# A hybrid layer on one core: a gate tile, RWKV's clamp and masks, and the start of attention change their place

## The chip, the cores and the metric

The kernel runs on one core of a Trainium2 chip, as one launch. The metric is the device time of one execution in microseconds, the median of some runs. The engines meant below are TensorE (PE: matmuls and transposes), VectorE (DVE), ScalarE (ACT), GpSimd (POOL) and SyncE (SP), which only issues transfers. Each engine takes its instructions in the order in which they were built; they wait for each other through semaphores.

## The reference

One decoder layer over 1024 tokens of width 1024, all in float32. Two mixers work beside each other on the same normalized input, are weighed by sigmoid gates, and a SwiGLU feed-forward follows:

```python
p = rmsnorm(x, norm1_g) @ w_in           # RWKV columns | q, k, v | indexer columns | 2048 gate columns
ya = rwkv7_mix(token_shift(p_rwkv, mu))  # 8 heads of 64, state carried over all tokens
yb = dsa_attention(q, k, v, q_idx, k_idx, w_idx)   # 8 heads, 256 keys chosen for each query
m  = sigmoid(ga) * (ya @ w_o_rwkv) + sigmoid(gb) * (yb @ w_o_att)
h  = x + m @ w_out
z  = rmsnorm(h, norm2_g); u = z @ w_ffn_in
out = rmsnorm(h + (silu(u_gate) * u_up) @ w_ffn_out, normf_g)    # 2816 inner columns
```

The lines above are a digest with shortened names. In RWKV the key is divided by its norm, `kk / maximum(norm(kk), 1e-12)`, ahead of the scan over tokens.

## The kernel before, in words

Everything is held transposed, channels on the partitions and tokens along a row, in two halves of 512 tokens. A float32 product is made of three matmuls in a faster format: each operand is split into a high part (a copy by ScalarE, `split`, L114) and the rest (a subtraction by VectorE, L115), and `mm3` (L140, L141, L145) adds high x high, high x low and low x high. One output tile of a projection from 1024 channels is thus 24 matmuls of 128x512. `mm3_last` (L156) orders them so that the last k tile of the activations is read last.

The order of TensorE is written by hand; the order of the other engines comes from a scheduler that goes by dependencies and priorities. Dense work stands as generators in a queue, `fill`, and `pump(n)` draws about n matmuls of it wherever the code of RWKV would leave TensorE without work; `ticks` does so in small portions. RWKV's first quarters have attention and gate projections as their filling, the later ones the merge and the feed-forward of the first half.

RWKV goes in four quarters q of 256 tokens. In each the key's squares are summed by matmuls (`sums`, L587), VectorE clamps the sums into `nq` (L604), TensorE turns them (L608), VectorE takes two columns of eight into `nr` (L610), POOL raises them to the power -0.5 (L614), and after a split and another turn (L619) ScalarE copies `nrT` (L621), which L627 spreads over the channels. Then 64 products of 64x128 (L682) are masked by VectorE into eight tiles `MT`, two for each chunk c of four (L686), and TensorE turns B and K (L701), which ScalarE copies into `NAT` (L704). The first block of each mask is inverted on VectorE (`W`, L720 and L722), goes through memory (`d_w`, L724) and comes back as `TT` (L733) and, turned, `TZ` (L736), which L750 and L771 use ahead of the scan.

`att0` makes the gates of the second half: sixteen tiles of 24 matmuls, `proj_gates(1, ...)`, of which the first 64 matmuls are drawn before attention over the first half (`attend(0, ...)`), the rest in turn with it. Attention loads keys (L1036), values (L1040) and queries (L1048) through POOL's queue, multiplies them (L1062), takes the row maximum on VectorE (L1064), turns the weights (L1076) and applies them to the values (L1086).

At q=2, ahead of the L682 products, `ready()` runs what is left in `fill`, gives the buffers of `u1` (the normalized input of the second half) back, opens `zp0`, and draws the first step of `merge(0)`: eight tiles of ya and yb (256 KB each) are read back over SP and split into yhi and ylo. From then on `fill` holds the products of the merge with w_o, which begin behind the L701 of q=2, then those with w_out and the feed-forward.

At the end of the first half the last group of the feed-forward's way out (`ffn_out`, group 2, six k tiles) writes into h and adds up its squares (`Rms.add`, L234 and L235); `finish_out` does the same for the second half, in two parts of 256 tokens. `Rms.columns` (L241, L244) sums over the channels by matmuls with ones, and `spread` (L254) brings the result onto all partitions.

Of the kernel before, what the change touches and what calls it, by code (L numbers as in the profile page):

```python
# [11 lines left out]
F32 = mybir.dt.float32  # L12
# [37 lines left out]
def block_kernel(ctx: ExitStack, tc: tile.TileContext, ins: dict, outT: bass.AP, stop=None, dbg=None):  # L50
# [65 lines left out]

    wq = [SY]
# [102 lines left out]

    class Rms:


        def __init__(self, h, tok=slice(0, HT)):
            self.h, self.tok, self.n = h, tok, (tok.stop - tok.start) // 128
            self.acc = tp.tile([128, HT], F32, tag="sacc", name="sacc", bufs=2)

        def add(self, k):
            n = 128 * self.n
            if k == 0:  # L230
                A.activation(self.acc[:, :n], self.h[:, 0, self.tok], AF.Square)
            else:
                sq = tmp()
                A.activation(sq[:, :n], self.h[:, k, self.tok], AF.Square)  # L234
                V.tensor_tensor(self.acc[:, :n], self.acc[:, :n], sq[:, :n], op=ALU.add)  # L235

        def columns(self, rs2=None):

            ss, n = mix(), self.n
            for t in range(n):  # L240
                T.matmul(ss[:, 2 * t:2 * t + 2], self.acc[:, t * 128:(t + 1) * 128], ones[:, 0:2],  # L241
                         start=True, stop=True)
            rs = cp.tile([128, 4], F32, tag="rs", name="rs", bufs=1)
            V.tensor_scalar(rs[:, :n], ss[:, 0:2 * n:2], 1.0 / D, 1e-6, op0=ALU.mult, op1=ALU.add)  # L244
# [282 lines left out]
    def rwkv(half, p, consts, ready=None):  # L527
# [5 lines left out]
        for q in range(2 * half, 2 * half + 2):  # L533
# [14 lines left out]
            pump((64, 36, 24, 34)[q])  # L548
# [50 lines left out]
            V.tensor_tensor(km, km, k, op=ALU.mult)  # L599
# [4 lines left out]
            V.tensor_scalar(nq.rearrange("p a b -> p (a b)"), ps, 1e-24, None, op0=ALU.max)  # L604
            pump(14)
            ps = mix()
            for t in range(2):
                T.transpose(ps[:, t * 128:(t + 1) * 128], nq[:, t, :], ident)  # L608
            nr = p.tile([128, 16], F32, tag="nr", name="nr")
            V.tensor_copy(nr.rearrange("p (t c e) -> p t c e", t=2, c=4),  # L610
                          ps[:, 0:256].rearrange("p (t c k) -> p t c k", t=2, c=4)[:, :, :, 0:2])
# [4 lines left out]
            pump((24, 26, 22, 26)[q])  # L616
# [4 lines left out]
            A.activation(nrT, ps[0:16, 0:256], AF.Copy)  # L621
            pump(10)
# [51 lines left out]
            for c in range(4):  # L674
                pr, pa = divmod(c, 2)
                m = p.tile([128, 8, 128], F32, tag=f"x{c}", name="MT")
                pss = [mix(), mix()]
                for hh in range(4):
                    for g in range(2):
                        h = 2 * hh + g  # L680
                        ct, ro = h // 2, slice((h % 2) * 64, (h % 2) * 64 + 64)
                        T.matmul(pss[g][:, hh * 128:(hh + 1) * 128],  # L682
                                 BK[ct // 2][ro, ct % 2, pr, 2 * pa:2 * pa + 2, :].rearrange("p s t -> p (s t)"),
                                 AR[ro, ct, c, :, :].rearrange("p s t -> p (s t)"), start=True, stop=True)
                for g in range(2):
                    V.tensor_tensor(m[:, g::2, :], pss[g].rearrange("p (h t) -> p h t", h=4),  # L686
                                    cmask[:, 64 - 64 * pa:192 - 64 * pa].unsqueeze(1).to_broadcast([128, 4, 128]),
                                    op=ALU.mult)
                MT.append(m)
                ba = 64 - 64 * pa  # L690
                for b in range(2):
                    i0 = (c * 2 + b) * 8
                    SY.dma_start(d_n[q][i0:i0 + 8].rearrange("h s t -> s h t"),
                                 m[ba + 32 * b:ba + 32 * b + 32, :, ba + 32 * b:ba + 32 * b + 32])
            NAT = []
            for pr in range(2):
                n = p.tile([128, 2, 512], F32, tag=f"x{4 + pr}", name="NAT")
                for pa in range(2):
# [5 lines left out]
                    A.activation(n[:, pa, :], ps, AF.Copy)  # L704
                NAT.append(n)

# [37 lines left out]
            ticks((211, 236, 281, 241)[q], (13, 4, 10, 6)[q])  # L744
# [520 lines left out]
    def ffn_out(half, zp, f, gi, sqs=None):  # L1265
# [42 lines left out]
    def finish_out(half, zp, f):  # L1308
# [6 lines left out]
        with tc.tile_pool(name="wf", bufs=8, side="left", reuse_waits="tile") as wf:  # L1315
            ws, before = [], None
            for o in range(0, HT, 256):
# [6 lines left out]
                for d in range(8):  # L1324
# [8 lines left out]
                    sq.add(d)  # L1333
# [24 lines left out]
    for half in (1, 0):  # L1358
        st, up = opened("left", f"up{half}")
        su.append(st)  # L1360
        us.insert(0, act_tiles(up, f"u{half}"))
# [38 lines left out]
    def att0():  # L1400
# [3 lines left out]
        gates = proj_gates(1, us[1], range(16))  # L1404
        for _ in range(16):
# [37 lines left out]
    sz0.close()  # L1443
    finish_out(1, zp1, f1[0])
# [80 lines left out]
```

## Time and profile before

| what | before |
|---|---|
| median of 3 runs | 1742.55 us (1739.08 to 1746.03) |
| profiled execution | 1741.15 us |
| its span | 1739.4 us |
| mean granted clock of TensorE | 0.993 |
| TensorE busy | 1706.6 us, 98% |
| VectorE busy | 1123.0 us, 65% |
| ScalarE busy | 846.9 us, 49% |
| GpSimd busy | 98.5 us, 6% |

The span is the time from the first to the last instruction in the trace. A row of a timeline gives start, duration, engine, line, operation, operands and count, and in brackets the idle time of the engine before it with what ended it. A row of the waits gives total, number of times and longest. Matmuls overlap, so from row to row the difference of the starts counts, not the duration of one. A row of the windows gives the busy time of each engine, then TensorE's granted clock, the share of busy DMA engines and GB/s. Profiled lines are those of the kernel before.

### The profile page before, as it was taken

The numbers are of one execution on the slowest core, as the hardware profiler recorded it, in microseconds if no ns is written. First come the engines' busy times: TensorE is split into PE (matmuls) and PEld (weight loads), VectorE is DVE, ScalarE is ACT, GpSimd is POOL, SyncE is SP. The second block draws the span as 40 slices with busy tenths as digits, with TensorE's granted clock in tenths as the row PEclk, the third lists the DMA queues.
The fourth block names the chain that finished last, engine by engine and source line by source line (L and its number), as shares of the span: only waits on it lengthen the run. The fifth ranks groups of instructions, "written<-read, shape, count | busy, mean of one in ns | idle before, by whom it ended". The sixth has DMA issues, their size and how long they took to land.

```text
span 1739.4 us, 26865 instructions
## 1 busy us (share of the span) xinstructions
PE 1706.6 (98%) x10156; PEld 1407.9 (81%) x10156; DVE 1123.0 (65%) x2189; ACT 846.9 (49%) x1627; POOL 98.5 (6%) x123
## 2 busy tenths in 40 slices
PE   8999999999999998999999999999999999999997
PEld 6888888778778777878788888888788888888887
DVE  6789989957567457957877655445566564454464
ACT  6355898553544688755334455533234332232241
POOL 0000000000021111001000311000000000000000
PEclk9999999999999999999999999999999999999998
DMA  5452334435357535643343864263464344434442
GB/s 211 155 154 85 98 108 146 158 96 174 104 180 202 147 113 164 202 147 118 104 122 116 237 159 132 69 222 110 164 218 135 100 146 154 136 96 149 136 128 86
DMA packets 144001, 247.16 MB, mean 142 GB/s; under 512 B 49232, under 2 KB 72464, under 8 KB 143744
## 3 DMA queue, kind: packets, MB, share of 16 engines
q1 hardware_dynamic: 120512, 171.61, 31.5%
q10 hardware_dynamic: 15552, 47.75, 8.6%
q0 software_dynamic: 7808, 26.09, 5.6%
q8 instruction: 80, 1.31, 0.3%
q14 instruction: 49, 0.40, 0.1%
HBM read 192.40 MB, written 53.00 MB: 141 GB/s over the span
## 4 chain that ended last, share of the span: by engine, by line
PE 78%; DVE 9%; ACT 6%; issue 3%; DMA 3%; POOL 0%; SPq 0%; ACTq 0%; DVEq 0%; POOLq 0%
PE acc L140 20%; PE acc L145 19%; PE acc L141 19%; PE acc L156 3%; PE mix L1086 2%; PE mix L1062 2%; PE mix L1076 2%; ACT junk L977 2%; DVE wlo L115 1%; ACT junkl L977 1%; PE mix L927 1%; DVE junk L974 1%; DMA wst<-in_w_ffn_in 1%; ACT whi L114 1%; PE acc L1230 1%
## 5 line engine op out<-in xcount | busy, mean ns | idle before, releaser
L115 DVE TENSOR_TENSOR wlo<-wst,whi 128x1024 fp32r<-128x1024 f32 (+1 forms) x229 | 276.2, 1209 | 275.2 <-PE acc L145 124.2
L114 ACT ACTIVATE whi<-wst 128x1024 fp32r<-128x1024 f32 (+1 forms) x229 | 238.1, 1042 | 232.5 <-PE acc L141 175.5
L140 PE MATMUL acc<-zhi,whi 128*128 128x512 f32 x672 | 264.7, 394 | 0.0
L141 PE MATMUL acc<-zlo,whi 128*128 128x512 f32 x672 | 262.0, 390 | 0.0
L145 PE MATMUL acc<-zhi,wlo 128*128 128x512 f32 x672 | 170.2, 392 | 0.0
L140 PEld LDWEIGHTS acc<-zhi,whi 128*128 128x128 f32 x672 | 126.2, 188 | 26.9 <-issue 1.7
L141 PEld LDWEIGHTS acc<-zlo,whi 128*128 128x128 f32 x672 | 126.2, 188 | 24.8
L145 PEld LDWEIGHTS acc<-zhi,wlo 128*128 128x128 f32 x672 | 124.7, 188 | 25.5 <-issue 0.7
L140 PE MATMUL acc<-u1hi,whi 128*128 128x512 f32 x352 | 141.0, 401 | 0.1
L141 PE MATMUL acc<-u1lo,whi 128*128 128x512 f32 x352 | 138.0, 392 | 0.0
L140 PE MATMUL acc<-u0hi,whi 128*128 128x512 f32 (+1 forms) x352 | 135.3, 387 | 1.8 <-DVE tmp L333 1.8
L141 PE MATMUL acc<-u0lo,whi 128*128 128x512 f32 (+1 forms) x352 | 133.7, 382 | 0.0
L140 PE MATMUL acc<-fhi,whi 128*128 128x512 f32 (+1 forms) x318 | 114.0, 367 | 2.0 <-ACT whi L114 1.0
L141 PE MATMUL acc<-flo,whi 128*128 128x512 f32 (+1 forms) x318 | 112.9, 364 | 0.2 <-DVE flo L115 0.2
L145 PE MATMUL acc<-u1hi,wlo 128*128 128x512 f32 x352 | 90.5, 397 | 0.0
L145 PE MATMUL acc<-u0hi,wlo 128*128 128x512 f32 (+1 forms) x352 | 86.5, 385 | 0.0
L114 ACT ACTIVATE fhi<-tmp 128x512 fp32r<-128x512 f32 x44 | 27.8, 631 | 114.1 <-DVE tmp L1262 114.1
L140 PEld LDWEIGHTS acc<-u0hi,whi 128*128 128x128 f32 x352 | 66.2, 188 | 15.3 <-ACT stg L114 2.2
L140 PEld LDWEIGHTS acc<-u1hi,whi 128*128 128x128 f32 x352 | 66.4, 189 | 14.4 <-issue 0.9
L145 PEld LDWEIGHTS acc<-u1hi,wlo 128*128 128x128 f32 x352 | 65.5, 190 | 14.0 <-issue 0.9
L141 PEld LDWEIGHTS acc<-u1lo,whi 128*128 128x128 f32 x352 | 66.5, 189 | 12.6
L141 PEld LDWEIGHTS acc<-u0lo,whi 128*128 128x128 f32 x352 | 66.2, 188 | 12.2
(330 smaller groups left out, 3223.4 us busy)
## 6 DMA issues: line engine op xcount, KB each, us to landing
wst<-in_w_ffn_in SPq DMA_DIRECT2D x72, 512.0 KB, 3.6
wst<-in_w_in ACTq DMA_DIRECT2D x36, 512.0 KB, 4.3
wst<-in_w_in SPq DMA_DIRECT2D x27, 512.0 KB, 3.9
wst<-in_w_fo SPq DMA_DIRECT2D x25, 512.0 KB, 4.0
k<-d_k POOLq DMA_DIRECT2D x24, 512.0 KB, 8.2
h<-in_xT SPq DMA_DIRECT2D x32, 256.0 KB, 5.2
d_g<-tmp ACTq DMA_DIRECT2D x32, 256.0 KB, 3.4
tmp<-d_g SPq DMA_DIRECT2D x32, 256.0 KB, 3.4
```

What stands on the lines that cost most here:

```text
L114: A.activation(hi, x, AF.Copy)
L115: V.tensor_tensor(lo, x, hi.bitcast(F32), op=ALU.subtract)
L140: T.matmul(ps, whi[:, wk + k, :], ahi[:, ak + k, tok], start=k == 0, stop=False)
L141: T.matmul(ps, whi[:, wk + k, :], alo[:, ak + k, tok], start=False, stop=False)
L145: T.matmul(ps, wlo[:, wk + k, :], ahi[:, ak + k, tok], start=False, stop=k == nk - 1)
L156: T.matmul(ps, w[:, k, :], a[:, k, tok], start=k == 0 and w is whi and a is ahi, stop=k == nk - 1 and a is alo)
L927: T.matmul(ps[:, :w], iq[:, h, :], ik[:, i, c:c + w], start=i == 0, stop=i == 1)
L974: V.tensor_scalar(junk[:, :n], y, z[:, i:i + 1], None, op0=ALU.is_ge, op1=ALU.add, accum_out=cnt[:, i:i + 1])
L977: A.activation(junka[:, :n], y, AF.Sign, bias=z[:, i:i + 1], accum_out=cnt[:, i:i + 1])
L1062: T.matmul(ps[:, :w], q[bi // 2][:, e, bi % 2 * 128:bi % 2 * 128 + 128], k[:, i, e, c:c + w], start=i == 0, stop=i == 1)
L1076: T.transpose(ps[:, j * 128:(j + 1) * 128], L[:, (c + j) * 128:(c + j + 1) * 128], ident)
L1086: T.matmul(py[64 * e:64 * e + 64, bi * 128:(bi + 1) * 128], v[:, j, 64 * e:64 * e + 64], pts[e][j // 4][:, j % 4, :], start=j == b, stop=j ...
```

## The change

1. The clamp `nq`, the copies `nr`, `nrT` and `NAT`, and the masks `MT` get a high priority in the scheduler (`urgent`), and the key multiply is put behind the clamp.
2. The numbers of the pumps in RWKV shift a little; in the second half (q=2 and q=3) there is a pump of two matmuls behind the masks of every chunk (`pump(2 * half)`; a step of filling is four, so it draws one behind the first and the third chunk), and the one ahead of the products grows from 10 to 14.
3. `att0` draws ten steps of gates (40 matmuls), not sixteen (64), before attention begins, and has fifteen gate tiles. The ticks of q=1 fall by 24.
4. The sixteenth gate tile goes behind `ready()`, ahead of the merge in `fill`, so that it lies among the products and turns of q=2 and beside the load of y. `u1` stays for so long, and its buffers become those of m, later f and z.
5. The merge splits the first four tiles of y in its first step and the last four in a second one, which the code of RWKV draws behind the last mask and the last NAT copy (`ready_y`).
6. The last group of `ffn_out` orders the matmuls of its first tile by `mm3_last`.
7. At the very end the last square isn't added by VectorE, but goes into the sums by matmuls of its own.

```diff
+    def urgent():
+        return tc.high_priority()
...
+    class Slots:
+        def __init__(self, pools):
+            self.pools = pools
+        def tile(self, shape, dt, tag, name):
+            return self.pools[tag].tile(shape, dt, tag=tag, name=name)
...
-        def add(self, k):
+            self.parts = [self.acc]
+        def add(self, k, last=False):
...
+            elif last:
+                self.parts.append(tmp())
+                A.activation(self.parts[1][:, :n], self.h[:, k, self.tok], AF.Square)
...
-            ss, n = mix(), self.n
-            for t in range(n):
-                T.matmul(ss[:, 2 * t:2 * t + 2], self.acc[:, t * 128:(t + 1) * 128], ones[:, 0:2],
-                         start=True, stop=True)
+            n, ps = self.n, self.parts
+            sss = [mix() for _ in range(n if len(ps) > 1 else 1)]
+            for x in ps:
+                for t in range(n):
+                    T.matmul(sss[t % len(sss)][:, 2 * t:2 * t + 2], x[:, t * 128:(t + 1) * 128], ones[:, 0:2],
+                             start=x is ps[0], stop=x is ps[-1])
...
-            pump((64, 36, 24, 34)[q])
+            pump((60, 36, 24, 34)[q])
...
-            V.tensor_tensor(km, km, k, op=ALU.mult)
...
-            V.tensor_scalar(nq.rearrange("p a b -> p (a b)"), ps, 1e-24, None, op0=ALU.max)
+            with urgent():
+                clamp = V.tensor_scalar(nq.rearrange("p a b -> p (a b)"), ps, 1e-24, None, op0=ALU.max)
+            with tc.issue_after(clamp.ins):
+                V.tensor_tensor(km, km, k, op=ALU.mult)
...
-            pump((24, 26, 22, 26)[q])
+            pump((28, 26, 22, 38)[q])
...
-            pump(10)
+            pump(10 if half == 0 else 14)
...
-                    V.tensor_tensor(m[:, g::2, :], pss[g].rearrange("p (h t) -> p h t", h=4),
-                                    cmask[:, 64 - 64 * pa:192 - 64 * pa].unsqueeze(1).to_broadcast([128, 4, 128]),
-                                    op=ALU.mult)
+                    with urgent():
+                        masked = V.tensor_tensor(
+                            m[:, g::2, :], pss[g].rearrange("p (h t) -> p h t", h=4),
+                            cmask[:, 64 - 64 * pa:192 - 64 * pa].unsqueeze(1).to_broadcast([128, 4, 128]), op=ALU.mult)
                 MT.append(m)
+                pump(2 * half)
...
-                    A.activation(n[:, pa, :], ps, AF.Copy)
+                    with urgent():
+                        last = A.activation(n[:, pa, :], ps, AF.Copy)
                 NAT.append(n)
+            if q == 2:
+                with tc.issue_after(masked.ins), tc.issue_after(last.ins):
+                    ready_y()
...
-            ticks((211, 236, 281, 241)[q], (13, 4, 10, 6)[q])
+            ticks((211, 212, 281, 241)[q], (13, 4, 10, 6)[q])
...
-        mt = act_tiles(zp, "m", ("s2", "s3"))
         for j in range(8):
             t = ylo[:, j, :].bitcast(F32)
             SY.dma_start(t, (d_ya if j < 4 else d_yb)[half][j % 4])
-            split(yhi[:, j, :], ylo[:, j, :], t)
-        yield -30
+        for j in range(4):
+            split(yhi[:, j, :], ylo[:, j, :], ylo[:, j, :].bitcast(F32))
+        yield -20
+        for j in range(4, 8):
+            split(yhi[:, j, :], ylo[:, j, :], ylo[:, j, :].bitcast(F32))
+        yield -10
+        mt = act_tiles(zp, "m", ("s2", "s3"))
...
-        pss = []
-        if not final:
-            pss = [acc(), acc()]
-            yield from mm3_last(pss, [w(d) for d in range(2)], f, gn)
+        pss = [acc() for _ in range(1 if final else 2)]
+        yield from mm3_last(pss, [w(d) for d in range(len(pss))], f, gn)
...
-                    sq.add(d)
+                    sq.add(d, last=d == 7 and o > 0)
...
-        gates = proj_gates(1, us[1], range(16))
-        for _ in range(16):
+        gates = proj_gates(1, us[1], range(15))
+        for _ in range(10):
             yield next(gates)
...
-        su.pop().close()
-        zps.append(opened("left", "zp0"))
-        m = merge(0, zps[0][1], z0)
+        sz, zp = opened("left", "zp0")
+        zp = Slots({"s0": zp, "s1": zp, "s2": up1, "s3": up1})
+        zps.append((sz, zp))
+        m = merge(0, zp, z0)
         next(m)
-        fill.append(chain(m, ffn(0, zps[0][1], z0, f0)))
+        zps.append(m)
+        fill.append(chain(proj_gates(1, us[1], range(15, 16)), m, ffn(0, zp, z0, f0)))
...
-    rwkv(1, rp, consts, ready)
+    rwkv(1, rp, consts, ready, lambda: next(zps[1]))
```

More of the change, by code (lines that the diff above doesn't have):

```diff
@@ L237, in columns @@
         def columns(self, rs2=None):
-            ss, n = mix(), self.n
-            for t in range(n):
-                T.matmul(ss[:, 2 * t:2 * t + 2], self.acc[:, t * 128:(t + 1) * 128], ones[:, 0:2],
-                         start=True, stop=True)
+            n, ps = self.n, self.parts
[4 more added lines that the diff above has]
+                             start=x is ps[0], stop=x is ps[-1])
             rs = cp.tile([128, 4], F32, tag="rs", name="rs", bufs=1)
-            V.tensor_scalar(rs[:, :n], ss[:, 0:2 * n:2], 1.0 / D, 1e-6, op0=ALU.mult, op1=ALU.add)
+            m = len(sss)
+            for t, ss in enumerate(sss):
+                V.tensor_scalar(rs[:, t:n:m], ss[:, 2 * t:2 * n:2 * m], 1.0 / D, 1e-6, op0=ALU.mult, op1=ALU.add)
             if rs2 is None:
@@ L525, in rwkv_consts, with rwkv @@
         return cmask, wup, gup, rmask, ind, ind16
-    def rwkv(half, p, consts, ready=None):
+    def rwkv(half, p, consts, ready=None, ready_y=None):
         cmask, wup, gup, rmask, ind, ind16 = consts
@@ L685, in rwkv @@
                 for g in range(2):
[L686 to L688 removed]
+                    with urgent():
+                        masked = V.tensor_tensor(
+                            m[:, g::2, :], pss[g].rearrange("p (h t) -> p h t", h=4),
+                            cmask[:, 64 - 64 * pa:192 - 64 * pa].unsqueeze(1).to_broadcast([128, 4, 128]), op=ALU.mult)
                 MT.append(m)
+                pump(2 * half)
                 ba = 64 - 64 * pa
@@ L703, in rwkv @@
                                     ident)
-                    A.activation(n[:, pa, :], ps, AF.Copy)
+                    with urgent():
+                        last = A.activation(n[:, pa, :], ps, AF.Copy)
                 NAT.append(n)
+            if q == 2:
+                with tc.issue_after(masked.ins), tc.issue_after(last.ins):
+                    ready_y()
             N = p.tile([128, 32, 32], F32, tag="x6", name="N")
@@ L1360, in block_kernel @@
         su.append(st)
-        us.insert(0, act_tiles(up, f"u{half}"))
+        us.insert(0, act_tiles(up, f"u{half}", ("s2", "s3") if half else None))
+        if half:
+            up1 = up
     sb, bp = opened("right", "bp")
```

7 lines of the change are left out of this document (4 added, 3 removed).

## The prediction

> **What bounds the kernel now.** I read the page first, then the waits of TensorE, then the timeline of each place that the change touches.
>
> ```profile
> span 1739.4 us, 26865 instructions
> ...
> PE 1706.6 (98%) x10156; PEld 1407.9 (81%) x10156; DVE 1123.0 (65%) x2189; ACT 846.9 (49%) x1627; POOL 98.5 (6%) x123
> ```
> ```profile
> PE mix L701 <- DVE MT L686: 3.3, 1, 3.3
> PE mix L682 <- DVE MT L686: 2.1, 3, 0.8
> ...
> PE mix L241 <- DVE sacc L235: 1.6, 1, 1.6
> ...
> PE mix L608 <- DVE nq L604: 1.0, 2, 0.9
> ```
>
> TensorE is busy all the time; its order is written by hand and the change leaves its work the same, so the time can only move by the stalls between matmuls, and these are few. The columns of the second view are total, number of times and longest. The four rows make 8.0 us, and all of them are waits that the change aims at. The largest stands where quarter q=2 of RWKV masks its products (line numbers are those of the kernel before):
>
> ```profile
> 674.70 1.16 PE L682 MATMUL mix<-AR,BK 64*128 64x128 f32 x16
> 676.63 2.88 PE L682 MATMUL mix<-AR,BK 64*128 64x128 f32 x34 [0.78 <-DVE MT L686]
> 680.23 1.16 PE L682 MATMUL mix<-AR,BK 64*128 64x128 f32 x14 [0.71 <-DVE MT L686]
> 684.68 3.68 PE L701 MATMUL mix<-kc,BK 128*128 128x128 f32 x16 [3.29 <-DVE MT L686]
> 688.00 0.78 PE L140 MATMUL acc<-yhi,whi 128*128 128x512 f32 x1
> ```
> ```profile
> 680.09 2.49 DVE L115 TENSOR_TENSOR ylo<-ylo,yhi 128x512 fp32r<-128x512 f32 x4
> 683.33 0.69 DVE L115 TENSOR_TENSOR ylo<-ylo,yhi 128x512 fp32r<-128x512 f32 x1 [0.75 <-ACT yhi L114]
> 683.94 2.48 DVE L686 TENSOR_TENSOR MT<-mix,cmask 128x512 f32<-128x512 f32 x4
> ```
> ```profile
> 682.67 0.63 ACT L114 ACTIVATE yhi<-ylo 128x512 fp32r<-128x512 f32 x1 [1.67 <-DMA ylo<-d_yb]
> ```
>
> VectorE runs in order. Four masks stand behind five y splits, and the fifth split waits, through ScalarE, for a y tile that is being read back. TensorE stands for 3.29 us meanwhile, with nothing else issued.
>
> **The change part by part.** *Masks of q=2, y splits and gate tile 15.* The yardstick is q=3, which does the same 64+16 matmuls without y splits, and for a dense matmul the row of sixteen from 519.62 on:
>
> ```profile
> 841.42 2.27 PE L682 MATMUL mix<-AR,BK 64*128 64x128 f32 x34
> 844.33 2.95 PE L682 MATMUL mix<-AR,BK 64*128 64x128 f32 x30 [0.64 <-DVE MT L686]
> 847.33 2.45 PE L701 MATMUL mix<-kc,BK 128*128 128x128 f32 x16
> 849.53 0.48 PE L140 MATMUL acc<-zhi,whi 128*128 128x512 f32 x1
> ```
> ```profile
> 517.78 2.00 PE L145 MATMUL acc<-u1hi,wlo 128*128 128x512 f32 x8
> 519.62 0.39 PE L140 MATMUL acc<-u1hi,whi 128*128 128x512 f32 x1
> ...
> 523.24 0.56 PE L1062 MATMUL mix<-k,q 128*128 128x128 f32 x4
> ```
>
> Sixteen dense matmuls take 523.24 - 519.62 = 3.62 us, 0.226 each, so the 24 of gate tile 15 take 5.4. Before, q=2 spends 688.00 - 674.70 = 13.3 us from first mask product to first y matmul, plus those 5.4 ahead of it: 18.7. q=3 needs 849.53 - 841.42 = 8.1 for the same products. After the change four gate matmuls (0.9 us) follow the products of c=0 and of c=2, which covers the 0.64 of q=3 and most of its shorter waits: 7.0, an estimate. Add the 5.4 and a remainder: in the built order two ylo splits still stand ahead of the masks of c=3, at 0.6 each (2.49 for four), 1.0 us taken, 0 to 2 kept. After: 13.4. Gain 5.3 (6.3 to 4.3). The upper four y splits now run after the masks and the NAT copies; they have 16 gate matmuls (3.6 us) and the first eight y matmuls (1.8) to hide under and need about four times 0.6 on ScalarE, then VectorE. I cost them at nothing; with the cover gone, 0 to 2 us.
>
> *Granted clock.* Part of those 13.3 us is TensorE at half clock: sixteen L701 took 688.00 - 684.68 = 3.3 us there, and 2.2 at q=3.
>
> ```profile
> 583.20:590.10 6.90, 6.20 (x179) 4.86 (x175) 2.81 (x6) 5.69 (x14) 0.00 (x0) 1.00 0.64 243
> 590.10:596.90 6.80, 6.80 (x40) 5.56 (x39) 1.59 (x6) 5.70 (x16) 1.20 (x2) 0.50 0.13 40
> 675.40:682.20 6.80, 4.45 (x58) 3.67 (x54) 6.31 (x11) 5.12 (x12) 0.00 (x0) 1.00 0.67 218
> 682.20:689.10 6.90, 4.42 (x19) 4.23 (x20) 5.54 (x10) 5.89 (x13) 0.00 (x0) 0.51 0.51 135
> ```
>
> Behind the five engines stands the granted clock: 0.51 from 682.2 to 689.1 and 0.50 from 590.1 to 596.9. I take it that the first goes with the gap and the second stays, which is what the sum above has; if the first stays, 1.1 on the L701 and up to half of 6.9 in all, 3.4, come back. The Trainium skill, "TensorE: Matmul & The Clock Gate", section Part 1, ties half clock to an idle window of about 3.4 us and asks for no gap above some 3. By that rule the stretch at 682 goes and nothing new comes, as summed; the trace agrees at 682 (3.29 idle) and not at 590, where the stretch before was busy for 6.20 of 6.90.
>
> *Clamp and nr copy in front (q=1, q=3).*
>
> ```profile
> 505.68 0.42 DVE L604 TENSOR_SCALAR nq<-mix 128x256 f32<-128x256 f32 x1
> ...
> 507.21 1.23 DVE L115 TENSOR_TENSOR wlo<-wst,whi 128x1024 fp32r<-128x1024 f32 x1
> 508.35 0.17 DVE L610 COPY nr<-mix 128x16 f32<-128x16 f32 x1
> ```
>
> The clamp now runs ahead of the key multiply, which has 1024 columns like the wlo split here (1.23 us), and of some shorter steps; the 1.0 of the L608 row goes (0.8 to 1.0). At q=3 a wait of the same kind, 0.2 to 0.3, goes too. Masks of q=3: the 0.64 and the shorter ones, 0.9 by the same four-matmul cover (0.5 to 1.3).
>
> *Attention 24 matmuls sooner.* The gate matmuls are only moved, so nothing is gained here; what can be lost is a wait of the first attention product (L1062) for its q. POOL loads it behind the pow of the nr chain:
>
> ```profile
> 508.68 2.92 POOL L614 TENSOR_TENSOR nr<-nr,mhalf 128x16 f32<-128x16 f32 x1 [2.30 <-DVE nr L610]
> ...
> 512.98 2.39 POOL L1048 DMA_DIRECT2D q<-d_q  x4
> ```
> ```profile
> DMA to landing us min/median/max: 6.0/6.1/8.0
> ```
>
> The first q lands at 512.98 + 6.1 = 519.1 and was used at 523.24. After, TensorE gets there at the place where 517.78 stands, less the 1.0 of the clamp: 516.8. The nr copy, ahead of the wlo split now, starts at about 507.2, so pow and loads come 1.1 sooner: 518.0, if the transfers speed up with their issue. The new wait is 1.2 to 2.3; I take 1.6, since k, v and weight loads share the engines. By the Trainium skill, "DMA: Bandwidth & Descriptors", Anatomy of one DMA (about 2.0 us plus bytes over 436 GB/s), these 128 KB would land in an estimated 2.3 us, there would be no wait and the sum would be 1.6 lower; the trace does not agree (6.0 at least).
>
> The same 24 matmuls are missing from the cover of the triangular inverse of q=1:
>
> ```profile
> 575.47 1.35 DVE L736 STREAM_TRANSPOSE TZ<-TT 32x256 f32<-32x256 f32 x3
> ```
> ```profile
> 583.82 1.20 PE L750 MATMUL mix<-TZ,MT 32*32 32x32 f32 x64
> ```
>
> TZ is ready at 576.8 and is used at 583.8: 7.0 spare, 5.4 less leaves 1.6. Behind the delayed masks of q=1 it may be late by 0 to 3; I take 0. Anything later than 1.6 costs one for one.
>
> *First tile of ffn_out (2) and the last norm.*
>
> ```profile
> 1241.24 0.39 PE L141 MATMUL acc<-flo,whi 128*128 128x512 f32 x1
> 1242.45 0.50 PE L140 MATMUL acc<-fhi,whi 128*128 128x512 f32 x1 [0.83 <-ACT fhi L114]
> 1243.18 0.50 PE L141 MATMUL acc<-flo,whi 128*128 128x512 f32 x1 [0.22 <-DVE flo L115]
> ```
> ```profile
> 1728.97 0.42 DVE L235 TENSOR_TENSOR sacc<-sacc,tmp 128x256 f32<-128x256 f32 x1 [0.54 <-ACT tmp L234]
> 1729.54 0.58 PE L241 MATMUL mix<-kc,sacc 128*128 128x2 f32 x4 [1.57 <-DVE sacc L235]
> ```
>
> Start to start the two waits are 1.21 and 0.73, less 0.226 each: 1.5. With fifteen matmuls of the first five k ahead of the last k instead of ten, all but 0.1 is covered: 1.4 (1.0 to 1.5). At the end 0.57 from the add to the sums falls away; one more small VectorE step and two tiny matmuls come: gain 0.3 (0 to 0.5). Weights, pools and the other pump numbers only shift dense work between places without a stall above 0.4: nothing, 0 to 0.5 either way.
>
> The sum: 5.3 + 1.0 + 0.2 + 0.9 + 1.4 + 0.3 = 9.1, less 1.6 = 7.5. The profiled run took 1741.15 us, 1.75 around its span; the median of the runs is 1.4 above that. 1742.55 - 7.5 = 1735.05, say 1735.0, 0.43% less than before. About 0.5% (8.7 us) is what a measurement of this kernel tells from no change, and the forecast lies just inside.
>
> **The rivals.** *Nothing is given back, and clock is gained.* If q lands in time (1.6) and the stretch at 590, which follows the small matmuls of q=1, falls on other work and goes (up to 3.4, half of 6.8), the gain is 12.5 at most; with one of the two 9.1 or 10.9: about 1732, faster. For it: no stall leads into 590. Against: the same small matmuls are still there.
>
> *Attention's early start eats more.* q not sooner (2.3), TZ three late: 0.7 + 3.0 off the gain, 3.8 left: 1738.7. For it: POOL's and SP's queues hold loads behind stores and pow; against: 1.6 spare. If the half clock at 682 stays instead, by 2 to 3.4, the time is 1737 to 1738.5.
>
> *The masks come no sooner.* If c=3's masks still end late, the 3.3 returns less 0.9 of cover: 1737 to 1738.
>
> *Slower: the urgent steps hold VectorE.*
>
> ```profile
> L686 DVE TENSOR_TENSOR MT<-mix,cmask x32: 680/682/692, 381.6 to 849.0; 128x512 f32<-128x512 f32 x32
> ```
>
> Thirty-two masks, four clamps and four copies stand further forward, each able to hold the in-order VectorE for its products while attention and splits wait behind it. To end over 0.5% slower, 7.5 + 8.7 = 16.2 us must reach TensorE, 0.4 for each of forty; at 0.6, the length of one split, 24 - 7.5 more than before gives 1759. Against: VectorE is 65% busy and the order moves each step by a few places.
>
> **How the numbers follow.** The central sum, 1732 to 1738: 0.48, of which 0.17 lies below 1733.8 (faster by over 0.5%) and 0.31 above. Nothing given back or clock gained: 0.23, faster. The three that eat into the gain, 1737 to 1743: 0.18, no change. Held VectorE or a stall I do not see: 0.11, slower. Faster 0.40, same 0.49, slower 0.11. The range leaves out the slower case and the far end of the best: 1729 to 1743.
>
> **What would show it.** After: no wait of L701 on a mask above 2 us, no wait of L608, a new wait of the first L1062 on q of about 1.6, L750 without one, no wait for fhi in ffn_out (2), clock full around the first y matmul. The prediction is wrong if L750 or the y matmuls stand for over 3 us, or if new half-clock stretches appear.

## The result, and the profile after

The changed kernel takes 1748.6 us in the median (1742.3 to 1755.2, 22 runs), the kernel before 1743.1 us (1738.2 to 1747.2, 22 runs). The ratio is 1.0029, 95% interval 1.0018 to 1.0041: 0.3% slower, which is less than 0.5% but clear of no change, and on the other side of the forecast. The forecast was 7.5 us faster; the medians are 5.5 us slower, 13.0 us apart from it. The profiled execution of the changed kernel took 1753.0 us with a span of 1751.3, at the long end of its runs; a second profile, of the fifth experiment below (e5), has a span of 1747.8 and waits at the same places. The lines of code have other numbers now: L1093 is the attention product (L1062 before), L707 and L728 are the mask products and the turns (L682, L701), L712 the mask (L686), L764 and L767 the loads of TT and the turns into TZ (L733, L736), L742 the load of N (L711), L1222 and L1226 the merge's gate load and its first step (L1187, L1191).

The waits of TensorE in the changed kernel (total, times, longest):

```profile
PE mix L1093 <- issue: 4.1, 1, 4.1
PE acc L144 <- DVE tmp L1226: 3.2, 1, 3.2
PE mix L1093 <- DVE mx L1095: 2.9, 1, 2.9
PE mix L874 <- ACT UV L865: 2.0, 3, 1.1
...
PE mix L802 <- DMA TT<-d_w: 1.2, 1, 1.2
PE mix L862 <- DVE rhs L853: 1.1, 1, 1.1
...
PE acc L144 <- DVE tmp L1293: 0.9, 1, 0.9
PE mix L643 <- DVE nr L115: 0.8, 1, 0.8
...
PE mix L260 <- ACT tmp L248: 0.7, 1, 0.7
...
PE mix L728 <- DVE MT L712: 0.4, 1, 0.4
```

The wait of 3.3 us before the turns is 0.4 now, the one for the clamp is gone, the last one fell from 1.6 to 0.7. In their place stand three waits of 2.9 to 4.1 us that weren't there, 10.2 us together. The first of them is for q: the view of the tile q puts the 4.1 us down to it, though the list says `issue`. Around q=3 there are three smaller ones that the kernel before doesn't have, in both profiles: 0.9 for the feed-forward's `tmp` (L1293) at 830.3, and 1.1 each for UV (the longest of L874's three) and rhs (L862) at 938.1 and 945.7, in the scan. The 0.64 at the masks of q=3 stayed. Around the masks of q=2 the timeline of TensorE is as full as foreseen:

```profile
677.89 1.16 PE L707 MATMUL mix<-AR,BK 64*128 64x128 f32 x16
...
680.11 2.06 PE L707 MATMUL mix<-AR,BK 64*128 64x128 f32 x32
...
686.25 0.66 PE L728 MATMUL mix<-kc,BK 128*128 128x128 f32 x4 [0.40 <-DVE MT L712]
...
690.39 0.39 PE L144 MATMUL acc<-yhi,whi 128*128 128x512 f32 x1
```

From the first product to the first y matmul it takes 690.39 - 677.89 = 12.5 us with the 24 gate matmuls inside, against 18.7 before: 6.2 gained; in the second profile it is 12.5 as well. But 11.6 us later, at the fourth block of the w_o products, TensorE stands. First TensorE, then VectorE, then SP's queue, all of the changed kernel:

```profile
701.94 0.50 PE L144 MATMUL acc<-yhi,whi 128*128 128x512 f32 x1 [3.22 <-DVE tmp L1226]
```
```profile
699.62 0.19 DVE L751 TENSOR_TENSOR tw<-W,N 128x31 f32<-128x31 f32 x1 [6.53 <-DMA N<-d_n]
...
701.20 0.68 DVE L1226 SCALAR_TENSOR_TENSOR tmp<-tmp,acc 128x512 f32<-128x512 f32 x1
```
```profile
691.75 1.09 SPq L742 DMA_DIRECT2D N<-d_n  x2
692.89 0.58 SPq L1222 DMA_DIRECT2D tmp<-d_g  x1
```

VectorE did nothing for 6.5 us: the first step of the triangular inverse stands ahead of the merge's step in its order and waits for N. In the kernel before the two loads had the other order on SP, and so had the two steps on VectorE (L1191 at 695.57, L720 at 701.04):

```profile
688.50 0.45 SPq L1187 DMA_DIRECT2D tmp<-d_g  x1
...
690.51 1.09 SPq L711 DMA_DIRECT2D N<-d_n  x2
```

The third new wait is in q=1, at the inverse's way back from memory (VectorE, then TensorE, in the changed kernel):

```profile
585.20 0.90 DVE L767 STREAM_TRANSPOSE TZ<-TT 32x256 f32<-32x256 f32 x2 [9.66 <-DMA TT<-d_w]
586.03 0.24 DVE L1095 CUSTOM_DVE_ANT_0 L<-mix,bias 128x128 f32<-128x128 f32 x1
```
```profile
586.35 0.51 PE L1093 MATMUL mix<-k,q 128*128 128x256 f32 x2 [2.88 <-DVE mx L1095]
```

VectorE stood for 9.66 us for TT, with attention's row maximum queued behind it. And at each of the three waits TensorE's granted clock (the number behind the five engines) falls to half, for 3.4 us or twice that. A fourth stretch follows a wait of only 1.21 us for TT at q=2 (L802, at 759.77):

```profile
519.20:526.00 6.80, 5.80 (x17) 4.96 (x18) 2.60 (x5) 0.77 (x3) 0.00 (x0) 0.50 0.88 227
587.40:594.30 6.90, 6.68 (x131) 5.52 (x133) 4.55 (x10) 5.83 (x15) 0.00 (x0) 0.51 0.55 175
703.50:706.90 3.40, 3.40 (x10) 2.63 (x9) 2.32 (x8) 2.41 (x3) 0.00 (x0) 0.50 0.64 250
```
```profile
761.50:764.90 3.40, 3.40 (x12) 2.50 (x10) 2.36 (x6) 1.09 (x4) 0.00 (x0) 0.50 0.04 14
```

The second one need not be new: the kernel before has a stretch of the same length at half clock at 590.1, with no long wait ahead of it, and that one is not there any more. The other three are new, 13.6 us of half clock, against the 6.9 at 682.2 that went. The difference of 6.7 us, at half clock, is worth at most 3.4 us, so among these places the waits are the larger part. The second profile has stretches of 3.4, 6.8 and 3.4 us, as much in all as the kernel before, and its span is still 8.4 us longer.

### The profile page after: what moved, and what is told of

Its sections match the earlier page's. It is cut to its first block, busy times and chain, and to the rows that moved or that the text cites. A ratio compares the mean times of both kernels' runs of the same rounds, so it can differ in the third digit from the quotient of the medians.

```text
span 1751.3 us, 26889 instructions
## 1 busy us (share of the span) xinstructions
PE 1709.8 (98%) x10160; PEld 1408.8 (80%) x10160; DVE 1122.1 (64%) x2189; ACT 846.7 (48%) x1627; POOL 101.3 (6%) x123
## 4 chain that ended last, share of the span: by engine, by line
PE 65%; DVE 6%; DMA 5%; ACT 2%; issue 1%; SPq 0%; POOL 0%; POOLq 0%; DVEq 0%; ACTq 0%
PE acc L144 17%; PE acc L149 17%; PE acc L145 16%; PE acc L160 3%; PE mix L1117 2%; PE mix L1093 2%; PE mix L1107 2%; DVE wlo L115 1%; DMA wst<-in_w_ffn_in 1%; DMA TT<-d_w 1%; PE acc L1265 1%; DMA N<-d_n 1%; DVE W L753 1%; PE mix L707 1%; DVE tw L751 1%
## 5 line engine op out<-in xcount | busy, mean ns | idle before, releaser
L145 PEld LDWEIGHTS acc<-u1lo,whi 128*128 128x128 f32 x352 | 66.6, 189 | 12.5
```

What stands on the lines that cost most here:

```text
L145: T.matmul(ps, whi[:, wk + k, :], alo[:, ak + k, tok], start=False, stop=False)
```

## The experiments

Ratios are to the kernel before on the same chip. "Changed" is the changed kernel of the first section.

| run | ratio | 95% interval |
|---|---|---|
| e1 changed, attention late again | 1.0048 | 1.0032 to 1.0064 |
| e2 before, attention soon alone | 1.0083 | 1.0066 to 1.0099 |
| e3 changed, first loads on SP | 1.0091 | 1.0068 to 1.0113 |
| e4 changed, inverse behind the merge on VectorE | 1.0044 | 1.0028 to 1.0060 |
| e5 changed, once more | 1.0035 | 1.0021 to 1.0050 |
| e6 before, priorities alone | 1.0012 | 0.9999 to 1.0025 |
| e7 before, the two parts at the end alone | 0.9997 | 0.9987 to 1.0008 |
| e8 before, priorities and end | 1.0009 | 0.9994 to 1.0023 |
| e9 before, masks of q=2 alone, and end | 0.9995 | 0.9981 to 1.0010 |
| e10 as e9, inverse and its load behind the merge's | 0.9979 | 0.9965 to 0.9992 |
| e11 changed, no priorities at q=3 | 1.0057 | 1.0037 to 1.0078 |
| e12 changed, k behind TT | 1.0015 | 0.9997 to 1.0033 |
| e13 changed, e12 and the order of e10 | 1.0026 | 1.0007 to 1.0045 |
| e14 as e10, another chip | 0.9966 | 0.9948 to 0.9984 |

### The early start of attention, undone and alone

```diff
 e1, in the changed kernel
-        for _ in range(10):
+        for _ in range(16):
-            ticks((211, 212, 281, 241)[q], (13, 4, 10, 6)[q])
+            ticks((211, 236, 281, 241)[q], (13, 4, 10, 6)[q])
 e2, in the kernel before: the opposite two lines
```

> The changed kernel with one part undone: attention begins after sixteen gate steps again (64 matmuls, ticks of q=1 back at 236); the moved gate tile, the priorities and the split merge stay. Theory A (the early start of attention costs the gain): the wait of the first attention product for q falls from 4.2 us to under 1, the TT loads of q=1 are issued some 5 us earlier against the attention's loads, so the 2.95 us wait behind TZ goes too, and with the half clock that follows each (some 3 us) the time falls by about 10 us to 1737 to 1740. Theory B (the loss sits at q=2, where VectorE stands for the load of N): the time stays within 3 us of 1748.6, and the 3.2 us wait of the w_o products for a merge step of VectorE stays.

> The kernel before with one part of the change alone: attention begins after ten gate steps (40 matmuls, ticks of q=1 at 212), all sixteen gate tiles still ahead of q=2. Theory A: the wait for q appears (3 to 4 us) and the TT chain of q=1 is late, 6 to 10 us slower than the kernel before, 1749 to 1753. Theory B: the early start is harmless by itself, within 2 us of 1743.

e2 came out on the side of theory A and beyond it, 1.0083: 15 us in the medians of its chip (1739.1 and 1754.2) where 6 to 10 were expected. The wait for q (1.8) and the late TT (3.3 for the row maximum) are there, and 4.3 us that nobody expected, before the turns of q=2, for a copy of NAT. e1 fits neither theory. The time doesn't fall, 1.0048, against A; and the wait at the fourth w_o block is gone from it without a gain, against B. The waits for q and for the row maximum are gone as well, and others came:

```profile
PE mix L707 <- DVE BK L677: 3.7, 1, 3.7
PE mix L1117 <- ACT pt L1109: 3.1, 2, 1.6
PE mix L802 <- ACT TZ L784: 2.5, 1, 2.5
```

The first two stand at 664 to 676, at the end of attention and at the first mask product of q=2, where the 24 gate matmuls had been; the third is in q=1 (587.2). As I read it, with the gate tile moved behind ready() and attention at its old place, attention ends too close to q=2, and VectorE and ScalarE are late there. So theory A falls in its simple form: the early start costs much by itself, but undone in the changed kernel it wins nothing.

### The first loads of attention on another queue

```diff
-            eng = G
+            eng = SY if half == 0 and hp == 0 else G
-                G.dma_start(q[...], d_q[...])
+                (SY if half == 0 and hp == 0 else G).dma_start(q[...], d_q[...])
```

> The changed kernel, with the first head pair's loads of k, v and q issued by SP instead of POOL, so that they no longer stand behind POOL's pow. If the queue behind the pow makes q late: q lands 3 us or more earlier, the first product waits under 1 us, the clock stays full there, all that follows in q=1 is 4 to 6 us earlier, 1740 to 1743. If the transfers themselves are slow because the DMA engines are full: the loads are issued earlier and land hardly sooner, a wait of 2.5 us or more stays, 1746 to 1749. Theory B expects no change in the total beyond 3 us either way.

q comes later, not sooner, the product waits longer, and 1.0091 is slower than either theory had it. The last line of the view of q (it shows the landing of one of the four transfers, issued at 513.0), and TensorE's row, in e3:

```profile
DMA to landing us min/median/max: 10.9/10.9/10.9
```
```profile
523.83 1.09 PE L1093 MATMUL mix<-k,q 128*128 128x128 f32 x4 [7.06 <-DMA q<-d_q]
```

In the changed kernel the same line says

```profile
DMA to landing us min/median/max: 7.4/8.4/8.6
```

with q issued behind the pow, all four transfers within 2.40 us from 511.18 on. SP issued the first two earlier, at 507.3 and 509.8, but spread the four over 9.81 us, and the product starts 3.6 us later. So leaving the pow out of the way by this queue wins nothing. Whether the pow costs anything on POOL's own queue isn't tested, since e3 changes the queue with it. That the DMA engines were full (share 0.88 in the window from 519.2 above) fits; that it is the whole reason isn't shown.

### The inverse's first step behind the merge, on VectorE alone

```diff
+            if q == 2:
+                pump(64)
             for l in range(31):
...
+                with tc.issue_after(mo[0].ins) if q == 2 and l == 0 else nullcontext():
-                V.tensor_tensor(o, W[...], N[...], op=ALU.mult)
+                    V.tensor_tensor(o, W[...], N[...], op=ALU.mult)
 mo holds merge's sums of the two gated parts, one a tile; the 64 come off the ticks of q=2
```

> The changed kernel with one order on VectorE changed: at q=2 the first step of the triangular inverse, which waits for the load of N, is put behind the merge step of the first w_o tile; the order of TensorE is the same. Theory B: the 3.2 us wait at the fourth w_o product block goes, with the half clock behind it (1.2 us), 1744 and no more than 1745. Theory A: it goes as well, but only these 4 us, and the loss in q=1 stays; if VectorE then stands for N a few steps later and TensorE with it, nothing is won, 1748.

The wait fell from 3.2 to 1.2 us and didn't go, a wait of 1.4 us for TZ of q=2 came, and nothing is won: 1.0044 is not apart from the changed kernel's 1.0035. VectorE no longer waits for N there but for the merge's own gate load, which SP issues behind N as in the changed kernel. e13 shows that with its lines, below. This profile also has 17.1 us of half clock from 581.6 on, in q=1, where the edit changes nothing.

### The changed kernel again

> The changed kernel as it is, a second look beside the single parts on one chip. If its loss comes from transfers that land late (q 8 us after its issue, TT 8.6 us, N 6 to 8 us), the waits stand at the same places with other lengths (1 to 5 us each), and the time lies 3 to 9 us above the kernel before. If the loss is one fixed order on VectorE, the waits repeat within 0.3 us.

1.0035. The waits stand at the same places: 1.9 for q (4.1 in the first profile), 3.6 for the merge's step (3.2), 3.4 for the row maximum (2.9). The order of all engines is the same in both, so the places go with the order; the lengths differ, and each of the three has a transfer at its root (q, N, TT).

### The parts one by one

e6 has the edits of `urgent()` alone, e7 those of the end alone (points 6 and 7 of the change), e8 both and the pump numbers outside q=2.

> The kernel before with the priorities alone (clamp, nr, nrT, masks, NAT, and the key multiply behind the clamp); no other number or place changes. Prediction's reading: the waits of L608 (1.0 us) and most of the 3.3 us before the L701 of q=2 go, 3 to 5 us faster, ratio 0.997 to 0.998. Rival (whatever comes early on VectorE makes later steps there wait for transfers, N at q=2 above all): the gain at the masks is given back behind the first y matmul, ratio 0.999 to 1.002.

> The kernel before with the last two parts alone: first tile of the last group of the feed-forward's way out by mm3_last, and the last square summed by matmuls. Nothing ahead of 1240 us changes. Prediction's reading: 1.4 us and 0.3 us gained, ratio 0.9990. Rival: the next step on the chain takes the wait over and the ratio is 1.000.

> The changed kernel without the early start of attention, without the moved gate tile and without the split merge; the priorities, the pump numbers outside q=2 and the two parts at the end stay. If the loss comes from the moved work alone (gate tile, attention, merge), this one has the gains without it: 5 to 8 us faster than the kernel before, ratio 0.9955 to 0.997. If the priorities themselves push VectorE into waits for transfers: ratio 0.999 or more.

e6 is the rival's case, 1.0012. Its waits have the masks' gain and its return side by side, and a new wait for the nr chain:

```profile
PE acc L144 <- DVE tmp L1201: 3.8, 1, 3.8
PE mix L626 <- DVE nr L115: 2.9, 2, 2.1
...
PE mix L710 <- DVE MT L695: 0.5, 1, 0.5
```

The 3.3 us before the turns became 0.5, and 3.8 us stand at the merge's step of the fourth w_o block, which had no wait before. e7 has neither wait for fhi, and 0.7 us instead of 1.6 at the last sum; its 0.9997 holds the expected 0.9990 and 1.000 alike. e8 is in the second case of its expectation, 1.0009: the expected gain isn't there even without the moved gate tile, the early attention and the split merge. Its wait at the fourth w_o block is 3.5 us.

### Masks of q=2 alone, with and without the order behind them

```diff
 e9, in the kernel before, with the end parts of the change
+                    with urgent() if q == 2 else nullcontext():       # masks MT and copies NAT, nothing else
 e10 and e14: e9, and
+            if q == 2:
+                pump(64)                                              # ticks of q=2: 217
...
+                with tc.issue_after(mo[0].ins) if q == 2 and l == 0 else nullcontext():
```

Here `mo[0]` is the low part of the merge's first m tile.

> The kernel before with the priority of the masks and NAT copies at q=2 alone, and the two parts at the end. Theory now: the masks gain 5 to 6 us up to the first y matmul, and VectorE gives 3.5 to 4 us of wait and 1 to 2 us of half clock back at the fourth block of the w_o products, where the inverse's first step stands in its order for the load of N; net 0 to 1 us there, 2 us at the end: ratio 0.9985 to 0.9995. Rival (the gain at the masks is lost by the priorities of other steps, clamp and nr at q=3): ratio 0.996 to 0.997.

> As the masks at q=2 alone, and the inverse's first step put behind the low part of the merge's first tile on VectorE; the order of TensorE is the same as in that kernel. Theory now: the wait at the fourth w_o block falls under 1 us and the gain at the masks stays, 4 to 6 us less than without this order: ratio 0.995 to 0.997 to the kernel before. Rival (the wait only moves on, to TT or TZ of q=2, since the inverse ends later): ratio as without it, 0.9985 to 0.9995.

> The kernel before with the masks and NAT copies of q=2 in front, the inverse's first step behind the merge's first tile, and the two parts at the end, on another chip: if its gain is of the order and not of that chip, ratio 0.997 to 0.999 again, and no wait above 1 us at the fourth w_o block; if not, 1.000.

e9 is as the theory had it. In e10 and e14 the wait at the fourth block is gone, as the theory had it, and the sizes came out otherwise: e10's 0.9979 lies between the theory's range and the rival's, and e14's 0.9966 just below the range that was expected after e10. In e9, TensorE, VectorE and SP:

```profile
698.57 0.70 PE L144 MATMUL acc<-yhi,whi 128*128 128x512 f32 x1 [3.09 <-DVE tmp L1214]
```
```profile
696.09 0.90 DVE L743 TENSOR_TENSOR tw<-W,N 128x31 f32<-128x31 f32 x1 [1.36 <-DMA N<-d_n]
...
697.84 0.68 DVE L1214 SCALAR_TENSOR_TENSOR tmp<-tmp,acc 128x512 f32<-128x512 f32 x1
```
```profile
690.26 1.08 SPq L734 DMA_DIRECT2D N<-d_n  x2
691.39 0.58 SPq L1210 DMA_DIRECT2D tmp<-d_g  x1
```

In e14, SP and VectorE:

```profile
682.78 0.45 SPq L1215 DMA_DIRECT2D tmp<-d_g  x1
...
684.41 1.13 SPq L734 DMA_DIRECT2D N<-d_n  x2
```
```profile
685.71 0.69 DVE L1219 SCALAR_TENSOR_TENSOR tmp<-tmp,acc 128x512 f32<-128x512 f32 x1
```

and TensorE around the masks of e14:

```profile
672.32 1.16 PE L703 MATMUL mix<-AR,BK 64*128 64x128 f32 x16
...
680.66 0.48 PE L144 MATMUL acc<-yhi,whi 128*128 128x512 f32 x1
```

Drawing the filling ahead of the inverse moved the gate loads ahead of N on SP as well as the step on VectorE; the merge's first step runs at 685.7, no wait is left at the fourth block, and the 13.3 us at the masks are 8.3 and stay gained (e9 has 8.3 there as well, and gives 3.1 back). The order of TensorE is the same in e9 and e10, and on the one chip that ran both the medians are 1742.4 and 1738.6 us. A little comes back later in e10 and e14: 0.9 to 1.4 us for whi at 736, where the kernel before has 0.5, and 0.7 for TZ at 744. e10 and e14 are the same kernel, on two chips 0.2% and 0.3% faster than the kernel before. It is the fastest found here, and faster than the kernel before and the changed one.

### No priorities at q=3

```diff
-        return tc.high_priority()
+        return nullcontext() if calm[0] else tc.high_priority()       # calm[0] is q == 3; pumps of q=3: 26, 10, 0
```

> The changed kernel, with the priorities, the pump of two matmuls and the larger pumps left out at q=3 alone. Theory now: q=3 costs the changed kernel 2 to 4 us (the nr chain and BK come late behind the steps in front), so the ratio falls from 1.0035 to between 1.001 and 1.002. Rival: the waits at q=3 move only to other places of its scan, ratio 1.003 to 1.004.

Neither theory: 1.0057, and a wait for the clamp of q=3 (2.3 us) in place of what was left out. So the priorities at q=3, taken out with the pumps, don't give the time back. The two waits of 1.1 us in the scan (UV and rhs) are gone here. e6, with the priorities and without these pumps, has neither; e8, with both, has three of 0.7 to 0.9. They go with the larger pumps at q=3. What else costs the changed kernel there stays open.

### The k loads behind TT, and both mends

```diff
 e12
-                    kqv[hp + 1] = load(hp + 1, sms[hp][:, 0, :] if half else None)
+                    late = TTs[-1][:, 0, 0, 0:2] if hp == 2 and not half else None
+                    kqv[hp + 1] = load(hp + 1, sms[hp][:, 0, :] if half else late)
```

`load` has POOL copy that piece into the k tile first, so the two transfers wait for the first TT tile. e13 has this and the order of e10 in the changed kernel.

> The changed kernel with one small copy added on POOL: the load of k for the last head pair, two transfers of 512 KB that the changed kernel issues 1 to 2 us ahead of the eight TT loads of q=1, now waits until the first TT tile has landed. All else, the order on every engine included, is as in the changed kernel. If TT lands late because it stands behind those k loads in the DMA engines: TT lands within 4 us of its issue instead of 8.6 to 9.5, the 3 to 3.4 us wait of the attention product behind TZ falls under 1 us, the half clock behind it goes, and the time falls by 4 to 6 us to a ratio of 1.000 to 1.002 to the kernel before. If TT is late for another reason (its own many small packets, the inverse ending late): the wait stays above 2 us and the ratio at 1.0025 to 1.0045.

> The changed kernel with both mends at once: k of the last head pair behind the TT loads of q=1 on POOL, and the inverse's first step at q=2 behind the low part of the merge's first tile on VectorE. If these two waits, and the half clock behind them, are what turned the expected gain into a loss: neither wait is left above 1 us, and the time falls 4 to 8 us below the changed kernel, ratio 0.998 to 1.000 to the kernel before. If each mended wait only comes back further on (TT, TZ or BK at q=2 and q=3): ratio 1.001 or more.

Issues of POOL and of SP in the changed kernel, the k load right ahead of TT, and the landing of TT:

```profile
574.40 1.24 POOL L1067 DMA_DIRECT2D k<-d_k  x2
```
```profile
576.53 8.97 SPq L764 DMA_DIRECT2D TT<-d_w  x8
```
```profile
DMA to landing us min/median/max: 1.8/6.3/8.7
```

and in e12:

```profile
573.06 4.62 SPq L765 DMA_DIRECT2D TT<-d_w  x8
```
```profile
578.94 1.25 POOL L1070 DMA_DIRECT2D k<-d_k  x2 [0.30 <-POOL k L1067]
```
```profile
DMA to landing us min/median/max: 1.7/3.0/4.3
```

With k held back, the median landing of TT falls from 6.3 to 3.0 us (2.1 in the kernel before, where TT is issued from 571.86 on, ahead of k at 574.40), and the wait of 2.9 us for the row maximum is gone from the list. That the two k loads made TT late is shown: the six profiles that have them just ahead of TT (changed, e2, e3, e4, e5, e11) give medians of 6.3 to 8.0 us, the two that hold them back 3.0 and 2.8 (e13). e12 is its first case, 1.0015; its worth in time isn't separated from the changed kernel's 1.0035, since the intervals overlap. e13 gives no more: 1.0026, its second case. 2.8 us are left at the fourth w_o block, and 2.6 us for TZ of q=2 are new. Its VectorE has the merge's step ahead of the inverse, and waits all the same:

```profile
696.14 0.69 DVE L1235 SCALAR_TENSOR_TENSOR tmp<-tmp,acc 128x512 f32<-128x512 f32 x1 [3.20 <-DMA tmp<-d_g]
```
```profile
687.49 1.09 SPq L742 DMA_DIRECT2D N<-d_n  x2
688.63 0.58 SPq L1231 DMA_DIRECT2D tmp<-d_g  x1
```

The order on VectorE was mended, that on SP not: the gate load still goes out behind N and lands some 7 us later. So the inverse's place on VectorE isn't all of it; e13 points to the two loads' place on SP as well. The kernel that has both in the old order and no wait is e10, and in the changed kernel itself the order on SP wasn't tried.

## Why the prediction was wrong, point by point

- **Masks of q=2, gain 5.3.** Right where it was measured (6.2), wrong that it stays. The step that failed is the path behind the masks, at which the sum has no term. The prediction asks there about the upper four y splits alone ("I cost them at nothing"), and these were in time. But with earlier masks the scheduler put N's load and step ahead of the merge's gate load and step. 3.2 us of wait (3.6 in the second profile) and 3.4 us at half clock follow. e6 and e9, without the moved work, have the wait too (3.8 and 3.1), e10 and e14, with the old order, haven't.
- **"I take 1.6" for the wait of q.** 4.1 in one profile and 1.9 in the other; 1.9 to 2.1 in e4, e12 and e13 and 2.8 in e11, which differ only further on. So four of six lie in its range of 1.2 to 2.3. The product needs two transfers, and the second landed 8.2 us after its issue in the first profile and 6.0 in the second. That the size mostly held is in part luck: the prediction counted on the first transfer and on a start 1.1 us sooner; it is the second, and the loads start 1.8 sooner.
- **TZ: "may be late by 0 to 3; I take 0".** 2.9 and 3.4 us, and not at L750, where the prediction looked, but at an attention product whose row maximum stands behind TZ on VectorE. The slack was counted in matmuls of cover, 7.0 less 5.4, as if TT would land as before. But two k loads went out ahead of TT now, and its median landing rose from 2.1 to 6.3 us. The rival "attention's early start eats more" had this wait with 3.0 us, and counted neither the half clock behind it nor what follows at q=2.
- **Granted clock.** The stretch at 682 went, as taken. That new waits bring others was not in the sum: 6.8 us at the wait for q, 3.4 behind the merge's step and 3.4 at 761.5. The stretch at 590 was taken to stay, and one of 6.9 us is at 587.4 now, behind the wait for the row maximum. The Trainium skill's rule ("TensorE: Matmul & The Clock Gate", Part 1, no idle gap above about 3.4 us) agrees with the stretches at waits of 4.1 and 3.2 us, and not with those of 3.4 us that follow waits of 1.21 (at 761.5) and 1.89 (q in the second profile). At 682.2 in the kernel before, half clock begins 0.8 us into the wait of 3.29, not behind it. Nor is a stretch a matter of the order alone. e7 has the same order as the kernel before on TensorE, VectorE, ScalarE and GpSimd up to 1239 us, and full clock around 590; e14 has it up to q=2, and full clock from 30 to 1720 us. The rows of e7 and of e14:

```profile
585.00:600.00 15.00, 13.52 (x245) 10.23 (x245) 6.06 (x17) 12.79 (x32) 1.20 (x2) 1.00 0.48 162
```
```profile
30.00:1720.00 1690.00, 1676.14 (x10064) 1383.85 (x10063) 1098.76 (x2135) 822.10 (x1590) 96.82 (x117) 1.00 0.47 141
```

Why 590 was slow in the one execution of the kernel before that was profiled stays open.

- **Clamp of q=1, gain 1.0.** The wait went, and a wait of 0.8 for the next step of the same chain, the split of nr behind the pow, took its place. POOL's pow took 3.76 us here (3.75 in e6, which has the priorities alone) instead of 2.92 (before, and e7), which is as much as the new wait. Why it took longer isn't shown.
- **q=3, gain 1.1, and the other pump numbers at "nothing, 0 to 0.5 either way".** The clamp's 0.2 went, the 0.64 of the masks didn't, and waits of 0.9, 1.1 and 1.1 came. The last two go with the larger pumps at q=3 (e6, e8 and e11 together), so that term was mis-sized, 2.2 us in place of at most 0.5. The 0.9 isn't in e8, which lacks the moved work.
- **End, gain 1.7.** The waits went as foreseen (1.6 to 0.7, and those for fhi); e7's interval is too wide to tell the time.
- **The slower rival.** It named VectorE held by urgent steps, but as forty small pieces. It was VectorE held, by two long waits for transfers.
- **Its own signs.** "The prediction is wrong if L750 or the y matmuls stand for over 3 us, or if new half-clock stretches appear." Both of the latter came: the product that stood for 3.2 us at the fourth w_o block is a y matmul.

Added up from the second profile, these terms make most of the 13.0 us between forecast and medians: 3.6 at the merge's step, 3.4 behind TT, 0.3 more for q, 3.1 at q=3, 0.9 not gained at its masks, 1.0 not gained at the clamps, less 0.9 that the masks of q=2 gave beyond 5.3: 11.4. That is an estimate, since waits don't simply add. What stays open is how much each makes in the median: the mends of two of them didn't add up.

## What to carry to other kernels

Before a step is put forward, list what the scheduler will put in the hole behind it, and ask of each of those steps which transfer it waits for and what the same in-order engine holds behind it; a wait that was taken away at one place came back here 12 to 16 us later with about the same size (3.1 to 3.8 us in the changed kernel, e6, e8 and e9), and stayed away only when both the step and its load were kept in their old order. Slack in front of a transfer is not a number of matmuls: ask which large transfer will be issued just ahead of it once the timetable shifts. A part that is tied to another (attention's early start to the gate tile's move) can't be judged by undoing it alone. And take a second profile before a wait or a stretch of half clock gets a price: the wait for q was 4.1 us in one and 1.9 in the other, with the same order on every engine.

## What the runs showed of the hardware

The same eight loads of TT landed in a median of 2.1 us ahead of two 512 KB loads and in 6.3 us behind them, in the traces of before and after. A 128 KB load of q, issued by POOL, landed after 6.1 us in the kernel before and 8.4 in the changed kernel (medians of the views). An estimate from the fit in the Trainium skill's "DMA: Bandwidth & Descriptors", Anatomy of one DMA, is 2.3 us; neither landing agrees with it. One issued by SP landed after 10.9 us (e3). POOL's pow of 16 columns took 2.92 us in the kernel before and 3.76 in the changed one. Between 30 and 1700 us, TensorE's half clock came in stretches of 3.4 us or about twice that (17.1 us once, in e4), most of them at waits of 1.2 us or more and some without (590.1 in the kernel before, with no gap above 0.4 us in the 6.9 us ahead), and it differed between profiles with the same order of the engines.
